# Two batches per output store, and three more transfers in the first load so that the last store takes the last completion semaphore

## Chip, cores, metric

One core of one Trainium2 chip. The metric is device time in microseconds (us); a time is the median of several executions unless said otherwise. "The kernel before" and "the changed kernel" are the two versions compared.

## The reference

```python
batch, m, k, n = 32, 512, 1024, 768
x:      (32, 512, 1024) float32
weight: (32, 1024, 768) float32
def reference(x, weight):
    return np.matmul(x, weight).astype(np.float32)
```

## The kernel before

Each batch is a 512 x 1024 by 1024 x 768 product. Weights and x are loaded and cast to bf16 by the GpSimd (POOL) queue; x comes two batches at a time, weights one at a time. PE transposes x, DVE and ACT copy the results from PSUM to an output tile, and the tile is stored. The parts that matter here:

```python
out_pool = ctx.enter_context(tc.tile_pool(name="out", bufs=7))     # one batch each: 128 x 3072 f32
...
x_first = x_pool.tile([P, MT - 1, K], F32, name="x_sb")            # batch 0, uncast, by the SP queue
x_fourth = out_pool.tile([P, 1, K], F32, name="out_sb")
nc.sync.dma_start(x_first, x_view[0, :, :MT - 1])
few = [slice(at, first + 20, 4) for first in (0, 20, 40) for at in range(first, first + 4)]
for rows in (slice(64, P), slice(60, 64), *few):                   # 1 + 1 + 12 transfers
    nc.sync.dma_start(x_fourth[rows, 0], x_view[0, rows, MT - 1])
# ... loads of the first weights and x ...
for b in range(B):
    # ... loads of later weights and x, 3 to 5 batches ahead ...
    if b <= B - LATE:
        if b > 0:
            pending.append(b - 1)
        if b % 2 == 0 and b + AHEAD < B - HELD or b == B - LATE:
            for at in pending:                                     # two stores at every even b
                nc.gpsimd.dma_start(out=out_view[at], in_=outs[at])
            pending = []
    if b == B - 1:
        # ... SP stores batches B-4, B-3 and the halves of B-2 ...
    outs[b] = out_pool.tile([P, MT * N], F32, name="out_sb")
    # ... transposes, matmuls, evacuation; SP stores the last batch in two halves ...
```

Two things are hidden in it. First, the framework gives each queue eight completion semaphores ("lanes") and deals them out in turn, so a transfer waits for the one eight before it on its queue. The end of the program waits for all lanes of SP's queue, one after the other. Second, 60 of the 128 rows of the last quarter of the first x are loaded in twelve transfers of five rows, which only five of the 16 DMA engines carry.

## Time and profile before

| | before |
|---|---|
| time, median of 3 | 515.02 us |
| span in the profile | 513.56 us |
| first DMA packet / last completion | 1.77 / 511.98 us |
| bytes | 167.77 MB read, 50.33 MB written |
| DMA share, 165 to 405 us | 1.02 |
| PE busy | 436.0 us (85%) |

How to read it: the compute engines have idle time, the 16 DMA engines have next to none between 4 and 509 us.

### The profile page before, as it was taken

How to read it: one execution, taken by the hardware profiler on the slowest of the kernel's cores; microseconds unless marked ns; L12 is line 12 of the kernel's file. 1: busy time of each engine (PE TensorE's matmuls, PEld its weight loads, DVE VectorE, ACT ScalarE, POOL GpSimd, SP SyncE). 2: the span in 40 equal slices, each digit the busy share in tenths (PEclk: the TensorE clock that was granted, in tenths of full speed). 3: DMA queues.
4: the chain of work that ended last, by engine and by line, in shares of the span. 5: the costliest groups of instructions: out<-in, count | busy, mean ns of one | idle time of the engine just before them, and what ended most of it. 6: DMA issues, size and time to landing. Idle time of an engine off the chain costs nothing.

```text
span 513.6 us, 5846 instructions
## 1 busy us (share of the span) xinstructions
PE 436.0 (85%) x2576; PEld 279.1 (54%) x2576; DVE 130.0 (25%) x196; ACT 76.2 (15%) x129; POOL 44.0 (9%) x87
## 2 busy tenths in 40 slices
PE   2808999999999798997979889898897989989990
PEld 1506666666666364654636546464563656656660
DVE  1205141323222141320414204141050422314120
ACT  0100211111111111111111111111111111110211
POOL 3000101001010101001010000100001101011000
PEclk9958999999999799998989979899897999999997
DMA  8999999999999999999999999999999999999997
GB/s 238 226 220 212 221 216 338 213 264 292 216 335 219 274 280 214 340 216 287 265 214 345 214 299 251 220 339 213 318 235 222 333 218 323 225 216 213 331 427 320
DMA packets 12904, 135.63 MB, mean 264 GB/s; under 512 B 1488, under 2 KB 1488, under 8 KB 3280
## 3 DMA queue, kind: packets, MB, share of 16 engines
q0 software_dynamic: 11664, 126.88, 96.5%
q1 hardware_dynamic: 1216, 8.39, 4.1%
q8 instruction: 20, 0.33, 0.2%
q14 instruction: 4, 0.03, 0.0%
HBM read 167.77 MB, written 50.33 MB: 425 GB/s over the span
## 4 chain that ended last, share of the span: by engine, by line
PE 39%; DMA 35%; issue 16%; DVE 4%; another core or an unknown queue 3%; POOL 1%; ACT 0%; POOLq 0%
PE pm L121 35%; DMA w_sb<-in_weight_dram 27%; DMA out_dram<-out_sb 6%; PE pt L76 4%; DVE xT L83 2%; DMA x_sb<-in_x_dram 2%; DVE out_sb L133 1%; POOL w_sb L68 0%; POOL x_sb L58 0%; POOL out_dram L167 0%; DVE xT L91 0%; ACT out_sb L134 0%; POOLq L167 0%; POOLq L68 0%
## 5 line engine op out<-in xcount | busy, mean ns | idle before, releaser
L121 PE MATMUL pm<-w_sb,xT 128*128 128x256 bf16 (+1 forms) x2048 | 354.0, 336 | 29.0 <-DMA w_sb<-in_weight_dram 29.0
L121 PEld LDWEIGHTS <-xT 128*128 128x128 bf16 x2048 | 205.3, 101 | 173.2 <-DMA w_sb<-in_weight_dram 32.8
L133 DVE COPY out_sb<-pm 128x512 f32<-128x512 f32 x64 | 44.3, 692 | 329.4 <-PE pm L121 306.1
L76 PE MATMUL pt<-ident,x_sb 128*128 128x128 f32 x496 | 79.7, 302 | 10.5 <-DVE xT L83 10.2
L76 PEld LDWEIGHTS pt<-ident,x_sb 128*128 128x128 f32 x496 | 69.2, 209 | 21.5 <-DVE xT L83 18.7
L83 DVE COPY xT<-pt 128x1024 bf16<-128x1024 bf16 x120 | 77.4, 687 | 11.0 <-PE pt L76 11.0
L132 ACT COPY out_sb<-pm 128x512 f32<-128x512 f32 x64 | 37.4, 585 | 282.3 <-PE pm L121 274.9
L134 ACT COPY out_sb<-pm 128x512 f32<-128x512 f32 x64 | 37.5, 586 | 143.4 <-PE pm L121 143.2
L68 POOL DMA_DIRECT2D w_sb<-in_weight_dram x37 | 19.8, 535 | 321.0 <-PE pm L121 307.7
L167 POOL DMA_DIRECT2D out_dram<-out_sb x28 | 15.0, 536 | 33.4 <-DMA w_sb<-in_weight_dram 25.4
L103 PE MATMUL pt<-ident,out_sb 128*128 128x128 f32 x8 | 1.9, 421 | 16.2 <-DMA out_sb<-in_x_dram 16.2
L103 PE MATMUL pt<-ident,x_sb 128*128 128x128 f32 x24 | 5.8, 422 | 10.2 <-DMA x_sb<-in_x_dram 10.2
L104 DVE CAST xT<-pt 128x512 bf16<-128x512 f32 x8 | 5.9, 732 | 31.9 <-PE pt L103 31.4
L58 POOL DMA_DIRECT2D x_sb<-in_x_dram x15 | 8.1, 540 | 67.0 <-DMA w_sb<-in_weight_dram 55.8
L103 PEld LDWEIGHTS pt<-ident,out_sb 128*128 128x128 f32 x8 | 1.6, 218 | 16.5 <-issue 16.5
L103 PEld LDWEIGHTS pt<-ident,x_sb 128*128 128x128 f32 x24 | 4.4, 214 | 11.2 <-issue 10.2
L91 DVE COPY xT<-pt 128x1024 bf16<-128x1024 bf16 x4 | 2.6, 686 | 0.2 <-PE pt L76 0.2
L132 ACT ACT_TABLE_LOAD x1 | 1.3, 1283 | 0.7 <-PEq L221 0.7
L62 POOL DMA_DIRECT2D x_sb<-in_x_dram x1 | 0.5, 527 | 6.8 <-DMA w_sb<-in_weight_dram 6.8
masks.py:199 POOL TENSOR_SCALAR_AFFINE_SELECT ident<-ident 128x128 f32<-128x128 f32 x1 | 0.3, 287 | 0.1
masks.py:197 POOL MEMSET ident<- 128x128 f32 x1 | 0.2, 223 | 0.0
L221 POOL MEMSET const-float32-0.0<- 128x1 f32 x1 | 0.1, 98 | 0.2 <-issue 0.2
(3 smaller groups left out, 0.3 us busy)
## 6 DMA issues: line engine op xcount, KB each, us to landing
w_sb<-in_weight_dram POOLq DMA_DIRECT2D x28, 1536.0 KB, 41.9
out_dram<-out_sb POOLq DMA_DIRECT2D x28, 1536.0 KB, 44.7
x_sb<-in_x_dram POOLq DMA_DIRECT2D x15, 2048.0 KB, 48.3
w_sb<-in_weight_dram POOLq DMA_DIRECT2D x7, 768.0 KB, 37.0
out_dram<-out_sb SPq DMA_DIRECT2D x4, 768.0 KB
out_dram<-out_sb SPq DMA_DIRECT2D x2, 1536.0 KB
x_sb<-in_x_dram SPq DMA_DIRECT2D x1, 1536.0 KB
x_sb<-in_x_dram POOLq DMA_DIRECT2D x1, 1024.0 KB, 36.2
```

The lines of the kernel that those rows point to most:

```text
L58: nc.gpsimd.dma_start(out=xs[b], in_=pair_view[b // 2])
L68: nc.gpsimd.dma_start(out=ws[b][:, at:at + n, :], in_=w_view[b, :, at:at + n, :])
L76: nc.tensor.transpose(pt[:, j, :], pairs[:, mo, j::JT], ident)
L83: nc.vector.tensor_copy(both[:, :, :, :, half, :].rearrange("p b j i r -> p j b i r"), words(b, mt + MT * half).rearrange("p j (b i r) -> ...
L91: nc.vector.tensor_copy(xT.rearrange("p j m r -> p (j m r)"), words(B - 1, mt).rearrange("p j m -> p (j m)"))
L103: nc.tensor.transpose(pt[:, i, :], rows[:, JT * h + i::KT], ident)
L104: nc.vector.tensor_copy(xT[:, 2 * h:2 * h + 2].rearrange("p j m r -> p j r m"), pt.rearrange("p (j r) m -> p j r m", r=2),)
L121: nc.tensor.matmul(pm[bank][:, at:at + size], xT[:, ko // 2, :, ko % 2], ws[b][:, ko, off:off + size], start=(ko == 0 and not (together an ...
L132: nc.scalar.copy(o[:, 0:512], pm[0])
L133: nc.vector.tensor_copy(o[:, 512:1024], pm[1])
L134: nc.scalar.copy(o[:, 1024:N2], pm[2])
L167: nc.gpsimd.dma_start(out=out_view[at], in_=outs[at])
```

## The change

The intent: 28 stores become 14 of twice the size, so there are fewer completions and more lanes to spare; and three more transfers for the first x (21 on the SP queue become 24) turn the lanes of the SP queue on by three, so that the last store takes the last lane and the end has nothing left to wait for after it. The memory for outputs stays the same (3 x 2 + 1 tiles in place of 7).

```diff
-    out_pool = ctx.enter_context(tc.tile_pool(name="out", bufs=7))
+    out_pool = ctx.enter_context(tc.tile_pool(name="out", bufs=3))
+    one_pool = ctx.enter_context(tc.tile_pool(name="one", bufs=1))
...
+    two_view = out.rearrange("(p r) (mi mo) n -> p mi r (mo n)", r=2, mi=P)
...
+    def open_out(b):
+        if b == B - 2:
+            outs[b] = one_pool.tile([P, MT * N], F32, name="one_sb")
+            return
+        if b % 2 == 0 or b == B - 1:
+            twos[b // 2] = out_pool.tile([P, 2, MT * N], F32, name="out_sb")
+        outs[b] = twos[b // 2][:, b % 2]
...
-        x_fourth = out_pool.tile([P, 1, K], F32, name="out_sb")
+        x_fourth = one_pool.tile([P, 1, K], F32, name="one_sb")
...
-        for rows in (slice(64, P), slice(60, 64), *few):
+        for rows in (slice(64, 96), slice(96, 112), slice(112, P), slice(60, 62), slice(62, 64), *few):
...
-                    for at in pending:
-                        nc.gpsimd.dma_start(out=out_view[at], in_=outs[at])
+                for at in pending:
+                    nc.gpsimd.dma_start(out=two_view[at], in_=twos[at])
```

(The stores stand at the same places of the program.)

More of the change, by code (lines that the diff above doesn't have):

```diff
@@ L48 @@
     out_view = out.rearrange("b (mi mo) n -> b mi (mo n)", mi=P)
-    xs, ws, outs = {}, {}, {}
+    two_view = out.rearrange("(p r) (mi mo) n -> p mi r (mo n)", r=2, mi=P)
+    xs, ws, outs, twos = {}, {}, {}, {}
     def banks():
@@ L161 @@
                 load_w(b + AHEAD)
-            if b <= B - LATE:
-                if b > 0:
-                    pending.append(b - 1)
-                if b % 2 == 0 and b + AHEAD < B - HELD or b == B - LATE:
-                    for at in pending:
-                        nc.gpsimd.dma_start(out=out_view[at], in_=outs[at])
-                    pending = []
+            if b % 2 == 0 and 0 < b < B - HELD - AHEAD:
+                pending.append(b // 2 - 1)
+            if b == B - LATE:
+                pending += [b // 2 - 2, b // 2 - 1]
+            if b + AHEAD < B - HELD or b == B - LATE:
+                for at in pending:
+                    nc.gpsimd.dma_start(out=two_view[at], in_=twos[at])
+                pending = []
             if b == B - 1:
@@ L174 @@
                 nc.sync.dma_start(out_view[b - 1, :, halves[1]], outs[b - 1][:, halves[1]])
-            outs[b] = out_pool.tile([P, MT * N], F32, name="out_sb")
+            open_out(b)
             if b == 0:
```

## The prediction

> **What bounds the kernel now.** I first read the busy lines and the DMA queues of the page, to see which resource has no idle time.
>
> ```profile
> PE 436.0 (85%) x2576; PEld 279.1 (54%) x2576; DVE 130.0 (25%) x196; ACT 76.2 (15%) x129; POOL 44.0 (9%) x87
> DMA  8999999999999999999999999999999999999997
> DMA packets 12904, 135.63 MB, mean 264 GB/s; under 512 B 1488, under 2 KB 1488, under 8 KB 3280
> q0 software_dynamic: 11664, 126.88, 96.5%
> HBM read 167.77 MB, written 50.33 MB: 425 GB/s over the span
> ```
>
> No compute engine is full, but the DMA row is at 9 in all but the first and the last slice. Next I cut the span into stages (columns: busy time and instructions of PE, weight load, DVE, ACT, POOL; granted clock; DMA share; GB/s).
>
> ```profile
> 2.00:45.00 43.00, 18.60 (x96) 12.55 (x97) 6.55 (x9) 1.78 (x4) 3.60 (x8) 0.80 1.01 234
> 45.00:165.00 120.00, 116.59 (x726) 77.10 (x725) 38.20 (x58) 20.98 (x36) 11.23 (x21) 1.00 1.02 255
> 165.00:405.00 240.00, 209.68 (x1195) 130.19 (x1193) 56.81 (x86) 35.22 (x61) 20.79 (x39) 0.92 1.02 268
> 405.00:487.00 82.00, 76.55 (x474) 49.83 (x473) 23.77 (x36) 13.46 (x23) 7.42 (x14) 1.00 1.03 251
> 487.00:502.00 15.00, 14.62 (x92) 9.39 (x90) 4.21 (x7) 2.92 (x6) 0.00 (x0) 1.00 1.01 427
> 502.00:512.00 10.00, 0.00 (x0) 0.00 (x0) 0.43 (x1) 0.54 (x1) 0.00 (x0) 0.77 0.85 356
> 512.00:513.60 1.60, 0.00 (x0) 0.00 (x0) 0.00 (x0) 0.00 (x0) 0.00 (x0) 0.50 0.00 0
> ```
>
> The DMA share is full (a hair over 1, because packets overlap in the records) in every stage from 2 to 502 us, whether PE is busy (45 to 165) or waits (165 to 405). So bytes set the end, not the waits of engines. The total is 167.77 + 50.33 = 218.1 MB. The first packet starts at 1.77 us and the last completion packet ends at 511.98: 510.2 us, or 427 GB/s. Only the ends are not full: 1.8 us before, 1.6 us after, and the stretch from 509 to 512 in which the 16 DMA engines stop one after another. The third view, the waits, shows what the issuing queue waits for in the steady stage (165 to 405 us):
>
> ```profile
> POOL w_sb L68 <- PE pm L121: 156.8, 15, 15.5
> POOL x_sb L58 <- DMA w_sb<-in_weight_dram: 51.8, 8, 6.6
> POOL out_dram L167 <- DMA w_sb<-in_weight_dram: 18.8, 8, 2.9
> ```
>
> The second and third line look like the prize: an x load or a store waits up to 6.6 us for an old weight load that it does not use. There are eight completion semaphores for this queue, and each transfer waits for the one eight before it. But the issue table says how far ahead of need this queue runs:
>
> ```profile
> w_sb<-in_weight_dram POOLq DMA_DIRECT2D x15, 1536.0 KB, 42.2
> out_dram<-out_sb POOLq DMA_DIRECT2D x16, 1536.0 KB, 45.5
> x_sb<-in_x_dram POOLq DMA_DIRECT2D x8, 2048.0 KB, 48.3
> ```
>
> A transfer lands 42 to 48 us after it is issued, in a queue that is served in order. Late issue costs nothing as long as that backlog is never used up. Last, the end, on the SP queue:
>
> ```profile
> SPq L232 <- DMA out_dram<-out_sb: 9.3, 5, 3.6
> L232 SPq EVENT_SEMAPHORE  x4: 28/28/28, 512.5 to 512.6; - x4
> ```
>
> SP waits for one semaphore after the other. In the records the last store lands at 512.01, SP sees it at 512.467 and then makes three more waits that have long been met, at 512.529, 512.588 and 512.649: about 61 ns each.
>
> **What the Trainium skill says.** (1) "DMA: Bandwidth & Descriptors", section "Where 436 GB/s comes from", gives a ceiling of 435.2 GB/s. The trace agrees: a weight packet reads 24,576 bytes and the next one starts 907 ns later on the same engine, which is 433.5 GB/s on 16. (2) The same page, "Why a DMA increments its semaphore by 16 and not by 1": a software-queue transfer posts a +1 from all 16 engines, a hardware-queue one only from the lowest-numbered k. The trace agrees in the counts: 81 software transfers x 16 = 1,296, plus 192 of the hardware queue (eight transfers on 16 engines, one on 4, twelve on 5), make the 1,488 packets under 512 B. (3) The same page, "Anatomy of one DMA", puts a fixed cost of about 2 us on a transfer, most of it the wait for the completion. Here the queue hides it: two neighbouring stores of 1.5 MB land 3.66 us apart, which is 8 packets x 457 ns = 3.656 us and 6 ns over. (4) "Perfetto Trace Analysis", section "What 'DMA-bound' means", names specific DMA engines as a possible bound. That fits: the 16 completions of the last store spread over 2.16 us.
>
> **The change part by part.**
>
> *Two batches per store.* 28 stores become 14, of the same bytes. The data packets stay what they are, 12,288 bytes each, since one batch's row of a partition is contiguous and the next batch's lies 1.5 MB on. The order of transfers on the queue stays x, w, w, out in each pair of batches. What goes is 14 completion packets on every engine at 6 ns of pitch (above): 14 x 0.006 = 0.08 us. I allow up to 0.2 us. 14 descriptor-making instructions of 0.536 us leave POOL, which is 9% busy: nothing on the path. POOL's lane waits mostly vanish, as eight semaphores now reach back two pairs of batches (four transfers each) rather than 1.6 (five each): x and stores are issued up to 6.6 us earlier into a queue that is 42 us deep: nothing.
>
> *Output buffers.* Seven single tiles become three doubles and one single of the same memory. A store is issued as before, when its second batch is done; its tile is needed again when batch b (even) is evacuated, four batches after the issue. From one first store of a pair to the next is 31.6 us at the median (165 to 405 us), so four batches are 63 us, plus about 8 to the first evacuation. The landing takes 46 us. Some 20 us of slack stay, so no new wait. For the last batch, the pair whose store landed at 490.0 must be out by 499.9: it is.
>
> *The first x in three more transfers.* The 64 rows become 32, 16 and 16, and 4 rows become 2 and 2. By the rule of k above, before, engines 0 to 3 carry one of the 4 rows each; after, engines 0 and 1 carry two and engines 2 and 3 none. A row is a packet of 172 ns. The twelve transfers of five rows already put 12 x 172 = 2.06 us more on five engines; in the completions of the load that lands at 41.5 us five of sixteen indeed trail by 2.0 to 2.5 us. So the end moves by +0.17, 0 or -0.17 us, as the last engine is 0 or 1, another, or 2 or 3; I can't tell, because records do not name engines. I take 0. Each hardware packet also waits its turn beside a load packet, so the last row, which lands at 39.5 us, comes some 2 us later. PE then starts the rest of batch 0 later. The lowest backlog behind it is at 61.6 us, where the last transfer in flight lands at 75.4: 13.8 us become about 12, still not idle, and the delay is gone when PE begins to wait for weights at 165 us.
>
> *The last lane.* The order of hardware transfers grows from 21 to 24 and the last store goes from the fifth lane to the eighth and last. Three waits of 61 ns after it go: 0.18 us, and these lie wholly on the path.
>
> Sum: -0.08 - 0.18 + 0 = -0.26 us; with the allowance for completion packets some -0.3. 515.02 - 0.3 = 514.7.
>
> **The rivals.** *Unlocked issue.* The 51.8 + 18.8 us of lane waits might be real delay, and their removal worth several us. For: they are the largest waits that the change touches. Against: the DMA share is 1.02 in that very stage. If I am wrong here it would be 505 to 510. *A new wait on the double tile,* or the queue filling up with more transfers in flight, would starve PE and then the loads; a stall of 2 to 10 us in total gives 517 to 525. Against it: the slack of some 20 us. *Imbalance.* Instruction fetches (20 of 16 KB, about 0.93 us each) fall on the engines in turn; if the shift of a few instructions puts one on the last engine, up to +0.9 us; if the other way, -0.5. That is the most likely way to miss the number. *Memory order:* a store that alternates between two batches could run slower than 457 ns a packet; 1% of 117 us of store time (32 x 8 x 457 ns) would be 1.2 us. The rate is the same for loads and stores, which speaks for a limit in the engine.
>
> **Range and chances.** The repeats of before lie within 0.06 us, so the range comes from the imbalance and the rows: 514.1 to 515.4. A gain of 2% (10.3 us) would need fewer bytes or a fuller queue, and there is neither; a loss of 2% needs a stall that the slack forbids. Faster 0.01, same 0.98, slower 0.01.
>
> **What would show it.** Packets under 512 B go from 1,488 to 67 x 16 + 224 = 1,296; the lane waits of x_sb and out_dram shrink to near nothing while the DMA share stays at 1.02 and the span hardly moves. No wait of SP stands between the one for the last store and the final drain. No evacuation waits for a store. The step "nothing on the path" is wrong if the stages' DMA share was below full in a way that these tenths hide, or if landings of stores move further apart than 7.32 us per pair.

## More of the kernel before

One more view will be needed: PE's timeline around the first batch (start us, length us, instruction, and in brackets the idle time before it and what ended it).

```profile
39.97 1.94 PE L103 MATMUL pt<-ident,out_sb 128*128 128x128 f32 x8 [16.18 <-DMA out_sb<-in_x_dram]
41.89 3.35 PE L121 MATMUL pm<-w_sb,xT 128*128 128x256 bf16 x16
45.08 1.12 PE L76 MATMUL pt<-ident,x_sb 128*128 128x128 f32 x8
```

PE sits idle for 16 us until the last row of that five-row load has come.

## The result, and the profile after

The changed kernel took 514.73 us (514.64 to 514.85, 4 runs) beside 515.05 us for the kernel before (4 runs). The ratio is 0.9993, with a 95% interval of 0.9976 to 1.001. Ratios are computed as the mean time of one kernel's runs over that of the other's of the same rounds, so not quite the ratio of the medians quoted. The interval of the ratio includes 1, no difference; the sign rests on the set of runs below.

From the page of the changed kernel, the line of the packets:

```profile
DMA packets 12712, 135.63 MB, mean 264 GB/s; under 512 B 1296, under 2 KB 1296, under 8 KB 3088
```

The packets under 512 B are 1,296 as forecast: 14 x 16 fewer from the stores, 32 more from the three more transfers of the first load. The stages (columns as in the prediction):

```profile
2.00:45.00 43.00, 15.44 (x81) 10.55 (x82) 5.79 (x9) 1.78 (x4) 3.64 (x8) 0.81 1.01 234
45.00:165.00 120.00, 116.63 (x713) 76.61 (x712) 38.19 (x58) 19.93 (x34) 9.83 (x17) 0.98 1.02 255
165.00:405.00 240.00, 211.58 (x1238) 133.30 (x1237) 59.50 (x91) 36.93 (x63) 19.11 (x33) 0.94 1.02 268
```

The DMA share and the rate of these stages are the same as before to the last digit: 1.01 and 234, 1.02 and 255, 1.02 and 268. What the POOL queue waited for from 165 to 405 us, and the stores and x loads of the issue table of the same stretch (KB each, median us from issue to landing):

```profile
POOL w_sb L70 <- PE pm L123: 226.3, 16, 15.5
POOL out_dram L179 <- issue: 2.6, 8, 0.6
```

```profile
out_dram<-out_sb POOLq DMA_DIRECT2D x8, 3072.0 KB, 48.1
x_sb<-in_x_dram POOLq DMA_DIRECT2D x8, 2048.0 KB, 57.1
```

The 51.8 + 18.8 us of lane waits are gone, and the wait for PE rose from 156.8 to 226.3 us: POOL waits as long as before, in another place. The x loads are issued earlier and land no earlier: 57.1 us from issue to landing instead of 48.3. (The load of batches 21 and 22, for one, has its last completion packet at 321.16 us before and 321.26 us after.) That is the whole fate of the biggest wait that the change removes.

All output copies of DVE waited for PE alone (the wait view of the whole run), and so did those of ACT, so the double tiles brought no wait for a store:

```profile
DVE out_sb L144 <- PE pm L123: 318.2, 62, 11.7
```

At the end, SP's waits from 512.1 to 512.3 us are one where there were four:

```profile
L244 SPq EVENT_SEMAPHORE  x1: 28/28/28, 512.2 to 512.2; - x1
```

And at the start, PE:

```profile
42.93 1.95 PE L105 MATMUL pt<-ident,one_sb 128*128 128x128 f32 x8 [19.06 <-DMA one_sb<-in_x_dram]
44.85 4.80 PE L123 MATMUL pm<-w_sb,xT 128*128 128x256 bf16 x16
49.50 1.12 PE L78 MATMUL pt<-ident,x_sb 128*128 128x128 f32 x8
```

PE goes on 3.0 us later (42.93 against 39.97), and by 49.50 it is 4.4 us late, because the 16 matmuls in between took 4.80 instead of 3.35 us: from 42.93 to 49.50 us the granted clock was 0.54, against 0.69 from 39.97 to 45.08 us before. The longer idle time is not the reason. In e10, the changed kernel once more, and in e1, with the first load as before, the same matmuls took:

```profile
44.86 3.31 PE L123 MATMUL pm<-w_sb,xT 128*128 128x256 bf16 x16
41.84 4.75 PE L123 MATMUL pm<-w_sb,xT 128*128 128x256 bf16 x16
```

The first line is e10, after 19.19 us of idle time, and the second e1, after 16.18 us. So 3.0 of the 4.4 us belong to the edit, and the rest differs between executions; what decides it is not shown. A delay of 4.4 us on the busiest compute engine, and the kernel is still faster: the clearest sign that PE is not the bound here.

The profiled spans are 513.56 and 513.08 us. Each is one execution. Taken apart at the last completion packet:

```text
from the trace's packet and semaphore records, us
                                          before    changed
last completion packet of all ends        511.982   511.810
SP sees the last store's semaphore        512.467   512.176
SP goes on after its last wait (drain)    512.714   512.241
end of the span                           513.556   513.078
```

Of 0.48 us, 0.17 lie before the last completion, and 0.18 are the three waits (from SP's sight to the drain, 0.247 and 0.065 us). The 0.17 cannot be put down to the edit: in e10, the same changed kernel, the last completion comes at 511.450 us, 0.36 us earlier than here. The 0.18 can: from sight to drain it is 0.247 or 0.248 us in all four profiles with three waits (before, and e1, e4 and e9 of the experiments below) and 0.065 us in all eight with the last store on the last lane. The other 0.12 is the time from the completion to SP's sight of it: 0.485 and 0.366 us here. Over all profiled runs it is between 0.34 and 0.49 us, with no relation to the edits that I could find, so I do not count it to the change.

### The profile page after: what moved, and what is told of

It reads as the page before. It is cut to its first block, busy times and chain, and to the rows that moved or that the text cites. A ratio compares the mean times of both kernels' runs of the same rounds, so it can differ in the third digit from the quotient of the medians.

```text
span 513.1 us, 5785 instructions
## 1 busy us (share of the span) xinstructions
PE 434.0 (85%) x2576; PEld 278.3 (54%) x2576; DVE 129.9 (25%) x196; ACT 76.3 (15%) x129; POOL 39.2 (8%) x73
## 2 busy tenths in 40 slices
DMA packets 12712, 135.63 MB, mean 264 GB/s; under 512 B 1296, under 2 KB 1296, under 8 KB 3088
## 4 chain that ended last, share of the span: by engine, by line
PE 46%; DMA 36%; issue 8%; DVE 6%; another core or an unknown queue 1%; POOL 1%; ACT 0%; SPq 0%; POOLq 0%
PE pm L123 41%; DMA w_sb<-in_weight_dram 28%; DMA one_sb<-in_x_dram 8%; PE pt L78 5%; DVE xT L85 4%; DVE out_sb L144 2%; PE pt L105 0%; POOL out_dram L179 0%; POOL x_sb L60 0%; POOL w_sb L70 0%; DVE one_sb L144 0%; DVE xT L93 0%; ACT out_sb L145 0%; SPq L151 0%
## 5 line engine op out<-in xcount | busy, mean ns | idle before, releaser
L144 DVE COPY out_sb<-pm 128x512 f32<-128x512 f32 x62 | 42.9, 692 | 318.2 <-PE pm L123 318.2
L78 PE MATMUL pt<-ident,x_sb 128*128 128x128 f32 x496 | 79.8, 302 | 10.4 <-DVE xT L85 10.1
L143 ACT COPY out_sb<-pm 128x512 f32<-128x512 f32 x62 | 36.3, 586 | 272.0 <-PE pm L123 272.0
L145 ACT COPY out_sb<-pm 128x512 f32<-128x512 f32 x62 | 36.3, 586 | 145.9 <-PE pm L123 145.8
L105 PE MATMUL pt<-ident,one_sb 128*128 128x128 f32 x8 | 1.9, 422 | 19.1 <-DMA one_sb<-in_x_dram 19.1
L105 PEld LDWEIGHTS pt<-ident,one_sb 128*128 128x128 f32 x8 | 1.6, 218 | 19.4 <-issue 19.4
L179 POOL DMA_DIRECT2D out_dram<-out_sb x14 | 10.0, 714 | 10.1 <-issue 3.7
L144 DVE COPY one_sb<-pm 128x512 f32<-128x512 f32 x2 | 1.4, 691 | 9.0 <-PE pm L123 9.0
L143 ACT COPY one_sb<-pm 128x512 f32<-128x512 f32 x2 | 1.2, 586 | 6.4 <-PE pm L123 6.4
L145 ACT COPY one_sb<-pm 128x512 f32<-128x512 f32 x2 | 1.2, 586 | 1.6 <-PE pm L123 1.6
```

What stands on the lines that cost most here:

```text
L78: nc.tensor.transpose(pt[:, j, :], pairs[:, mo, j::JT], ident)
L105: nc.tensor.transpose(pt[:, i, :], rows[:, JT * h + i::KT], ident)
L143: nc.scalar.copy(o[:, 0:512], pm[0])
L144: nc.vector.tensor_copy(o[:, 512:1024], pm[1])
L145: nc.scalar.copy(o[:, 1024:N2], pm[2])
L179: nc.gpsimd.dma_start(out=two_view[at], in_=twos[at])
```

## The experiments

Three groups, each on one chip with its own runs of the kernel before: e1, e2, e3, e5; then e4, e6, e7, e8; then e9 to e11. All results were correct. "Difference" is the mean of the runs minus the mean of the kernel before in the same group, with one standard error worked out from the spread of both (nine runs of the kernel before in each group, five of each other, four of e4).

| run | stores | rows per engine | lane of the last store | median us | difference us |
|---|---|---|---|---|---|
| changed (first result) | double | moved | last | 514.73 | -0.36 ± 0.08 |
| e10: changed again | double | moved | last | 514.63 | -0.35 ± 0.09 |
| e1 | double | as before | fifth, as before | 514.87 | -0.12 ± 0.13 |
| e2 | single | moved | last | 514.72 | -0.20 ± 0.09 |
| e5 | double | moved | first | 515.17 | +0.16 ± 0.10 |
| e3 | double | as before | last | 514.42 | -0.49 ± 0.08 |
| e11: e3 again | double | as before | last | 514.48 | -0.43 ± 0.06 |
| e8 | single | as before | last | 514.77 | -0.31 ± 0.08 |
| e9 | in column halves | as before | fifth | 516.52 | +1.68 ± 0.13 |
| e4 | in partition halves | as before | fifth | 525.16 | +10.4 ± 0.3 |
| e6 | double | level | last | 516.26 | +1.28 ± 0.25 |
| e7 | double, two tiles | moved | last | 537.76 | +23.0 ± 0.3 |

### The parts alone: e1 and e2

e1 is the changed kernel with the first x loaded as before:

```diff
-        for rows in (slice(64, 96), slice(96, 112), slice(112, P), slice(60, 62), slice(62, 64), *few):
+        for rows in (slice(64, P), slice(60, 64), *few):
```

> The changed kernel with the first x loaded as before: two batches per store alone, the last store on the fifth lane. Theory (sum of small terms): 14 completion packets per engine fewer, 0.08 to 0.2 us, so 0.05 to 0.25 us under the kernel before; SP makes three met waits after the one for the last store. Rival (unlocked issue: the lane waits were real delay): the whole gain of 0.3 us or more is here, and e2 shows none.

e2 is the kernel before with only that line changed the other way.

> The kernel before, with only the first x in three more transfers: the last store on the last lane, single stores. Theory: 3 waits of 61 ns fewer after the last store, 0.18 us, plus or minus 0.17 us for the rows that move from engines 2 and 3 to 0 and 1: 0.0 to 0.35 us under the kernel before; from the landing of the last store to the end of the span some 0.2 us less. Rival (all gain from the stores): no difference, or 0.1 us slower for three more completion packets and the later start of PE (as in the changed kernel, some 4 us later).

Measured: -0.12 and -0.20 us; together -0.32 against -0.35 for both. So the times lean to a split. The rival that put all of the gain on freed issue wanted 0.3 us or more in e1, which frees the lanes of the POOL queue, and none in e2; it fits worse, but e1's error is as large as its effect, and the times alone do not exclude it. Against it speak the x loads that land no earlier, and e9 below. In e1 SP still made four waits at the end (window 511.6 to 511.94 us):

```profile
L244 SPq EVENT_SEMAPHORE  x4: 28/28/28, 511.7 to 511.9; - x4
```

### The lane, made worse: e5

```diff
-        for rows in (slice(64, 96), slice(96, 112), slice(112, P), slice(60, 62), slice(62, 64), *few):
+        for rows in (*(slice(at, at + 16) for at in range(64, P, 16)), slice(60, 62), slice(62, 64), *few):
```

One transfer more, the same rows on each engine: the last store falls on the first lane.

> The changed kernel with one transfer more (64 rows as four of 16, the rest as in the change): the last store falls on the first lane, so SP makes seven more waits after it. Theory: 7 x 61 ns = 0.43 us slower than the changed kernel, all between the landing of the last store and the end. Rival (the lane does not matter, or all lanes are waited for at once): the same as the changed kernel.

Measured: 0.51 us slower than the changed kernel (+0.16 against -0.35, both relative to the kernel before), where 0.43 was expected. SP's waits after the last store, window 512.1 to 512.66 us:

```profile
L244 SPq EVENT_SEMAPHORE  x8: 28/28/28, 512.2 to 512.6; - x8
```

One for the store and seven more. From SP's sight of the store to the drain it is 0.494 us (512.154 to 512.648) against 0.065: 0.43 us for seven, 61 ns each. This part is shown in the records. By the times the lane may be worth more, but their errors do not decide it: e3 below, which differs from e1 only in the cut of the 64 rows and so in the lane, is 0.37 ± 0.15 us faster than e1, where three waits give 0.18.

### The rows: e3, e8, e11

The three more transfers can also be had without moving a row from one engine to another:

```diff
-        for rows in (slice(64, 96), slice(96, 112), slice(112, P), slice(60, 62), slice(62, 64), *few):
+        for rows in (*(slice(at, at + 16) for at in range(64, P, 16)), slice(60, 64), *few):
```

> The changed kernel, last lane kept, but the three more transfers are made by cutting the 64 rows in four (16 each) and the four rows stay one transfer, so each engine carries the same rows as in the kernel before. Theory, with rows that do not matter: the same as the changed kernel within 0.1 us. If engine 0 or 1 ends last in the changed kernel: up to 0.17 us faster. If engines 2 or 3 were the last: 0.17 us slower.

> The kernel before, single stores, with the first x in three more transfers that leave the rows of each engine as they were (64 rows as four of 16): the last store on the last lane, no row moved. Theory (lane 0.18, the moved rows cost 0.17, two per store gives 0.1): 0.2 to 0.4 us faster than the kernel before, and 0 to 0.3 us faster than the kernel before with the rows moved. Rival (the gain of the rows seen with double stores was noise): the same as that kernel within 0.05 us.

> The changed kernel with the rows of each engine as in the kernel before (64 rows as four of 16, last lane kept), the fastest so far, beside the changed kernel: theory, up to 0.3 us faster than the changed kernel. Rival (it was run-to-run drift): the same within 0.1 us.

e10 is the changed kernel itself, for the same chip as e11:

> The changed kernel itself, for the comparison with the next on one chip: 0.2 to 0.4 us faster than the kernel before.

With double stores, e3 is 0.13 us faster than the changed kernel (-0.49 against -0.36, each beside its own runs of the kernel before), and on one chip e11 is 0.08 faster than e10; with single stores, e8 is 0.11 faster than e2. Three comparisons, one sign, about 0.1 us, but each with an error of 0.10 to 0.12 us. That would agree with a term of at most 0.17 us for the two engines that carry one row more in the changed kernel, but it is not shown: e2, with the rows moved, already gains the whole 0.18 us of the lane, which leaves nothing for the rows to cost, and it is e8 that gains 0.13 us more than the lane gives. No record names the last engine. e3 is the fastest version found, at 514.42 and 514.48 us.

The same table gives the stores once more: with the rows kept, e3 and e11 against e8, -0.46 against -0.31: 0.15 us; with the rows moved, -0.355 against -0.20: 0.155; and 0.12 in e1, each with an error of about 0.1.

The packet records are finer here. From the completions of the transfer before a pair of stores to those of the pair, taken engine by engine in order of time, it is 7.313 us at the median in each of the three profiled kernels with single stores (before, e2, e8) and 7.307 us in each of seven with double stores (changed, e1, e3, e5, e6, e10, e11). The completion packet that a pair saves is worth 6 ns, as predicted, and 14 of them 0.08 us.

### Are lane waits on the path? e4 and e9

e4 goes the other way with the kernel before, to twice as many stores:

```diff
-                        nc.gpsimd.dma_start(out=out_view[at], in_=outs[at])
+                        for part in (slice(0, 64), slice(64, P)):
+                            nc.gpsimd.dma_start(out=out_view[at, part], in_=outs[at][part])
```

> The kernel before, with each of its 28 software-queue stores made as two transfers of 64 partitions: 28 transfers more, the same 12,288-byte packets, and each transfer now waits for the one eight before it with seven transfers in a pair of batches instead of five. Theory (bytes set the end, a completion packet costs some 6 ns of pitch): 0.1 to 0.4 us slower than the kernel before, with much longer lane waits of the POOL queue (over 100 us in total) and a DMA share that stays full. Rival (lane waits are real delay): several us slower, as lane waits double.

Measured: +10.4 us. My expectation of 0.1 to 0.4 us failed, and the rival's "several us" was met in number. But the packet records show another reason: the packet time of an engine, summed, rose from 516.6 to 525.8 us. Packets of 12,288 bytes, of weights and stores together, took 318.2 instead of 311.4 us per engine (3,723 instead of 3,591 of them over 600 ns), x packets 148.6 instead of 147.3; so it was not the stores alone that became slower. The DMA share from 165 to 405 us was full, at a lower rate:

```profile
165.00:405.00 240.00, 203.91 (x1170) 127.13 (x1168) 56.74 (x86) 34.65 (x60) 27.62 (x51) 0.91 1.02 259
```

So the engines were not idle, they were slower. The edit had changed two things at once, and a second run was needed that cuts the stores and leaves each transfer all 128 partitions:

```diff
-                        nc.gpsimd.dma_start(out=out_view[at], in_=outs[at])
+                        for part in (slice(0, N2), slice(N2, 2 * N2)):
+                            nc.gpsimd.dma_start(out=out_view[at, :, part], in_=outs[at][:, part])
```

> The run with stores cut into partition halves was 10 us slower, but its store packets themselves took longer, so it did not separate the theories. Here each of the 28 stores of the kernel before is cut by columns instead: two transfers of all 128 partitions, 6,144-byte packets, each engine writing as before. Seven transfers in a pair of batches, so lane waits several times those of the kernel before. Theory (lane waits cost nothing while the queue is backed up): 16 packets at a pitch of some 231 ns instead of 8 of 457 ns are 40 ns more, plus 6 ns for a completion, by 28: 1.3 us slower, DMA share full. Rival (lane waits are real delay, or it was they that cost the 10 us): 5 to 12 us slower again.

Measured: +1.68 us by the means, +1.56 by the medians, near the 1.3 of the theory and far from 5 to 12. The waits of POOL from 165 to 405 us, those for a transfer only, and the stage:

```profile
POOL w_sb L68 <- DMA x_sb<-in_x_dram: 75.1, 8, 9.5
POOL w_sb L68 <- DMA w_sb<-in_weight_dram: 53.8, 8, 6.7
...
POOL out_dram L168 <- DMA w_sb<-in_weight_dram: 20.5, 3, 6.9
POOL out_dram L168 <- DMA out_dram<-out_sb: 19.8, 15, 1.4
POOL x_sb L58 <- DMA out_dram<-out_sb: 7.0, 7, 1.0
```

```profile
165.00:405.00 240.00, 208.52 (x1203) 130.29 (x1201) 56.81 (x86) 35.76 (x61) 28.29 (x54) 0.93 1.02 266
```

176.2 us of such waits against 70.6 before, two and a half times as many, with a DMA share still at 1.02. The cost agrees with that of the smaller packets and of the added completions. So more than a hundred us of added lane waits are off the path here; that their removal is worth nothing rests on the x loads above. Why partition halves make packets slower stays open: I did not separate how 64 partitions are spread over the engines from the order in which they come.

### Is an early PE start worth anything, and do engines end unevenly? e6

```diff
-        for rows in (slice(64, 96), slice(96, 112), slice(112, P), slice(60, 62), slice(62, 64), *few):
+        for rows in (slice(0, P),):
```

> The changed kernel with the fourth quarter of the first x in one transfer of 128 rows, so each of the 16 engines carries 8 rows: engines 0 to 4 lose some 8 rows (1.4 to 1.7 us), the other eleven gain 4 (0.69 us). The last store is still on the last lane (8 transfers). Theory (the end is the last of 16 engines, and both groups end near each other): 0.2 to 0.7 us slower than the changed kernel, with the first of the 16 last completions earlier and the spread wider, though PE starts batch 0's last quarter some 25 us earlier. Rival (an early PE start matters): faster than the changed kernel by 0.5 us or more. If engines 0 and 1 alone set the end: faster.

PE's first batch goes on as soon as its work before is done, 19.4 us before the changed kernel (23.53 against 42.93):

```profile
23.53 1.05 PE L105 MATMUL pt<-ident,one_sb 128*128 128x128 f32 x8
```

and the kernel is 1.6 us slower than the changed one (+1.28 against -0.36). The last 16 completions show where the time goes:

```text
completions of the last store, us after the first of the 16 engines
changed: 0.00 0.02 0.36 0.59 0.62 0.77 0.82 1.05 1.09 1.40 1.46 1.49 1.49 1.85 1.87 2.21   (first: 509.60)
e6:      0.00 0.07 0.38 0.67 1.28 1.56 1.62 1.74 1.77 1.84 1.85 1.92 3.47 3.59 3.69 3.70   (first: 509.02)
```

With level rows four engines trail the rest by 1.5 us. So it seems that the five-row transfers, which look wasteful at the start, give five engines more bytes to make up for something that later falls on others; the likely cause are the 20 instruction fetches of 16 KB, about 0.93 us of an engine each, but the records do not name engines, so this is argued and not shown. The direction was as expected, the size was not: 1.6 us against my 0.2 to 0.7. The runs spread more as well, from 515.74 to 517.00.

### Does a wait for a store reach the end? e7

```diff
-    out_pool = ctx.enter_context(tc.tile_pool(name="out", bufs=3))
+    out_pool = ctx.enter_context(tc.tile_pool(name="out", bufs=2))
```

> The changed kernel with two double output tiles instead of three: the store of a pair must land within some 40 us of its issue (two batches of 15.8 us and 8 us to the first evacuation) instead of 71, against 46 to 50 us measured. Theory: evacuations wait for the store, PE falls back by up to 10 us, and transfers are issued later, so the backlog shrinks (landing times of 35 to 42 us) but the DMA share stays full: the time stays within 0.5 us of the changed kernel. Rival (a wait on the store is on the path): 8 to 12 us for each of 12 pairs is partly lost, 5 to 50 us slower.

Measured: +23 us; my expectation of no change failed. The waits of ACT for stores, from 60 to 440 us and then from 440 us to the end:

```profile
ACT out_sb L143 <- DMA out_dram<-out_sb: 131.4, 11, 13.9
```

```profile
ACT out_sb L143 <- DMA out_dram<-out_sb: 33.1, 1, 33.1
```

and the stages:

```profile
165.00:405.00 240.00, 207.41 (x1227) 135.87 (x1224) 57.09 (x86) 32.55 (x59) 19.11 (x33) 0.92 1.02 268
405.00:460.00 55.00, 46.57 (x277) 30.53 (x278) 15.84 (x24) 8.80 (x16) 4.96 (x9) 0.94 1.02 245
460.00:487.00 27.00, 6.94 (x45) 4.52 (x43) 0.00 (x0) 0.00 (x0) 0.73 (x1) 0.69 1.04 268
500.00:510.00 10.00, 10.00 (x63) 6.08 (x62) 1.38 (x2) 2.34 (x4) 0.00 (x0) 1.00 0.00 0
```

Both theories were half right. Eleven waits, 131 us in all, cost nothing: up to 487 us the DMA share is full at the rate of the changed kernel, and the last weight load that comes as one transfer, whose first completion comes at 428.6 us in the changed kernel, has it at 428.5 here. The twelfth wait causes the loss. The last stores are held back behind the last loads, so batch 28 (with two tiles) waits from about 456 to 489 us for a store that is in line behind all of them; PE idles, the loads run out, and from 500 to 510 us the DMA engines have nothing to do. Between 487 us and the last completion at 534.4 us each engine is idle for some 23.5 us, about as much as the loss. The three double tiles and the single one of the change are just enough that the last batches need no held-back store but one: that store landed at 489.8 us, about 10 us before its tile was needed.

## Why the prediction was right

- **Bytes set the end.** Right. Share and rate by stage did not move, and the stages of e9, and of e7 up to 487 us, stay full under far greater waits.
- **The lane, 0.18 us.** Right: 0.182 us in the two profiles, 61 ns a wait also in e5. (One reading was off: the prediction has the last store land at 512.01 us; the last record of its semaphore is at 512.450, 17 ns before SP sees it.)
- **Completion packets, 0.08 us, up to 0.2.** The 6 ns a piece, and so the 0.08 us, are shown by the pairs of stores (7.313 and 7.307 us), though the prediction's own sum, 3.66 less 3.656, gave 4. The time says 0.12 to 0.155 us in three comparisons, with errors of about 0.1, so it shows neither that there is more nor that there is not.
- **The rows, taken as 0 out of +0.17, 0 or -0.17.** Open. The times lean to a cost of up to 0.1 us, within their errors.
- **The sum.** -0.26 to -0.3 us was forecast, and -0.36 ± 0.08 and -0.35 ± 0.09 measured: 514.7 against 514.73. The records show 0.18 + 0.08 = 0.26 us of it. That the time agrees with the forecast to 0.03 us is partly luck: the last completion of one and the same kernel moves by 0.36 us between two profiles, and if the moved rows did cost 0.1 us, some 0.2 us of the gain would have no explanation.
- **PE some 2 us later, backlog 12 us.** Too small: 4.4 us, and the lowest backlog was 9.4 us (at 66.0 us, the last transfer in flight landing at 75.4). The step that was mis-sized is the row's turn beside the loads: the row came 3.0 us later, not 2, in both profiles of the changed kernel. The other 1.4 us are the slower matmuls of this one execution; in e10 PE is 2.9 us late (48.01 against 45.08). It did not matter, as the same step said.
- **The rival "unlocked issue".** Wrong as ruled: the waits went, and came back as a wait for PE. (POOL was relieved of 4.8 us of work, not of 14 x 0.536 = 7.5, as the instruction for a double store takes 0.71 us; it is not on the path.)
- **The rival "new wait on the double tile", 2 to 10 us for a stall of 2 to 10.** It did not come about. Its arithmetic was wrong, however: e7 shows that eleven stalls in the middle were free and that the one behind the last loads, of 33.1 us, cost 23 us. The place of the wait counts more than its length.
- **The rivals "imbalance" and "memory order".** Neither shows: the last 16 completions spread over 2.21 us against 2.16, and a store of two batches is not slower than two stores. That instruction fetches fall on the engines in turn was assumed; no record names an engine.

## What to carry to other kernels

When the DMA engines are full in every stage, expect, as here, that the removal of waits on the issuing side moves the wait elsewhere and leaves the end where it is; look for what sets the end in bytes, in packets and in what comes after the last completion. The order in which the program's end waits for semaphores is worth a look, since here each met wait after the last store's cost 61 ns, and the number of transfers alone removed them. When transfers go to a part of the DMA engines, check which engines get the rows, and before buffers are merged check above all the last few tiles, where in e7 no backlog hid the wait.

## What the Trainium skill lacked or had wrong

- "DMA: Bandwidth & Descriptors", section "Anatomy of one DMA": its fit with a fixed 2.0 us per transfer would promise 28 us for 14 transfers fewer, if it were applied to a full queue. Here they brought 0.08 us by the records (6 ns each) and about 0.15 us, with an error of 0.1, by the time. The section does say that most of the 2 us is completion latency and that the semaphore write itself is nearly free; it does not say what is left of the fixed cost in a queue that is always full.
- The same page, "Rules for kernel authors": it says that two transfers to disjoint partition halves serialize and are not worth the bother. The runs show more than that, a loss: stores cut into partition halves cost 10.4 us over 28 stores, with slower packets, where cutting the same stores by columns cost 1.7.
- "Runtime: NRT & Kernel Launch", section "Instruction fetch mechanics", calls the cost of crossing a 16 KiB block mostly hidden. Here 20 fetches of 16 KB stand in the DMA records at about 0.93 us each, by an estimate from that 1.2 us per engine if spread evenly; in a kernel in which the DMA engines are never idle they add to the work. Whether they are what makes engines end 2.2 us apart is not shown.
- I found no page with the cost of a wait for a semaphore that is already met at the end of a program on SP: 61 ns.
